# Weight sums of the input projections: stored from GpSimd's results for the second half, instead of made by adding transfers

## The chip, the cores and the metric

The kernel runs on one core of a Trainium2 chip. The metric is device time in microseconds of the slowest core, here the only one. Five engines work side by side, each in the order of its own queue: TensorE (PE in the profile, with its weight loads as PEld), VectorE (DVE), ScalarE (ACT), GpSimd (POOL) and SyncE (SP). SP, ACT and POOL also issue transfers, which 16 shared DMA engines carry out. A transfer issued by POOL can add its data to what lies at the destination; the kernel uses such adding transfers from DRAM to DRAM.

## What is computed

One layer of a hybrid trunk over 2048 positions of width 1024, in float32. Cut to what matters here:

```python
xn = rmsnorm(x, norm1_g)
z = xn @ w_in                      # pool | q | forget | input | output gate | branch gates
u_pool, zq, zf, zi, zo, zg = split(z)
gates = sigmoid(zg + b_gate)
ya = pool_mixer(u_pool) @ w_pa     # trailing means, per group a 128x128 product
yb = hgrn2_mixer(zq, zf, zi, zo) @ w_pb   # gated linear recurrence over chunks
x = x + (gates[0] * ya + gates[1] * yb) @ w_o
h = causal_conv3(rmsnorm(x, norm2_g) @ w_up)
x = x + (silu(gate_half(h)) * value_half(h)) @ w_down
out = rmsnorm(x, final_g)
```

## The kernel before

The sequence goes through in two halves of 1024 positions (b0 = 0 and b0 = 2), each as two blocks of 512. In each half the stages follow each other: the projections of the values and output gates ("io"), the other input projections in 14 units ("in": forget and q, branch gates, pool channels), the recurrence beside them in its own tasks, the two branch products (pa, pb), the output product (wo), the up product with its convolution and gating (up, 22 units), and the down product (dn).

The large products use a form of Strassen's scheme with seven half-size products, P1 to P7, in place of eight. P1, P2 and P4 take a quarter of the weights as it stands; P5, P6, P7 and P3 take sums and differences of quarters, called s1 to s4. Both operands are split into a rounded part and its remainder (ACT casts, VectorE subtracts), and three matmuls are made per pair; so every weight operand is one load into a raw buffer (line 183, on SP), a cast on ACT (L205) and a subtraction on VectorE (L206) into an operand buffer. There are 8 raw buffers and 6 operand buffers; loads run ahead as far as the raw buffers allow, conversions up to 4 operands ahead.

Where the sums s1 to s4 come from differs by half. The weights of wo, up and dn get their sums from adding transfers throughout: `Sums.make` takes a group of up to four units and issues eight transfers per group, four plain ones on ACT (L267) and four adding ones on POOL (L264), each of n x 256 KB for n units. `prepare` is a task that runs the groups two at a time, some seven ticks between the steps of a group, from the end of the first io stage on. A tick is six matmuls in program order, so the adding transfers spread over the first half. The input projections are needed first, before any such sums can be there: in the first half they load the quarters and add them on GpSimd (L373 for the "in" units, L315 for "io", there partly on VectorE). For the second half, `prepare` makes their sums again by transfers, as its last five groups: so0 (four units of io), si0, si1, si3 (four units each) and si2 (two units). Each sum in DRAM is then loaded like a quarter.

In the down product, POOL also issues the loads of its activations (g, L777) and of the residual rows (ac, L777), while SP issues the weight loads, then at its end the rows of x for the next half (L482) and the results (L1430). ACT squares those rows of x (L607) and casts the activations (dn_P, L578) in one queue.

The order of instructions on each engine is set by a scheduler from the program's text; so a change in one place moves neighbours elsewhere a little. The scheduler also gives every transfer one of eight completion counters: SP and ACT share eight, POOL has eight of its own. A transfer waits until the one eight places ahead of it on its set of counters has landed.

Of the kernel before, what the change touches and what calls it, by code (L numbers as in the profile page):

```python
# [11 lines left out]
F32 = mybir.dt.float32  # L12
# [6 lines left out]
P = 128  # L19
# [8 lines left out]
MF = D_FF // P  # L28
# [51 lines left out]
def tile_trunk(  # L80
# [77 lines left out]
    class Stream:  # L158
# [34 lines left out]
        def convert(self):  # L193
            j = len(self.tiles)
            key, fn, raws = self.ops[j]
            while any(r.tile is None for r in raws):
                self.load()
            v = fn(f"w{j}")
            t = opsp.tile([P, 2, 512], F32R, tag="ops", name=f"ops{j}")
            n = int(np.prod(v.shape[1:]))  # L200
            hi, lo = t[:, 0, :n], t[:, 1, :n]
            if len(v.shape) == 3:
                hi = hi.rearrange("p (a b) -> p a b", a=v.shape[1])
                lo = lo.rearrange("p (a b) -> p a b", a=v.shape[1])
            self.mark = act.copy(hi, v)  # L205
            dve.tensor_tensor(lo, v, f32(hi), ALU.subtract)  # L206
            self.tiles.append((key, t))
            self.load_ahead()
# [70 lines left out]
    def grouped(src, mv, mg, names):  # L279
# [7 lines left out]
        return names, [part(mv, 0), part(mv, 1), part(mg, 0), part(mg, 1)]  # L287

    def plan_one(key, src):
        r = stream.raw(src)  # L290
# [4 lines left out]
    def plan_io(b0):  # L295
        for p in IO_ORDER:
            for k in range(4):
# [6 lines left out]
                if b0:  # L304
                    plan_one("io", sums["io"].of(k, SUM_OF[p]))
                    continue
                use = {"P6": (2, 3, 0), "P5": (2, 3), "P7": (2, 0), "P3": (2, 3, 0, 1)}[p]
                raws = [stream.raw(q[i]) for i in use]

                def fn(nm, p=p, raws=raws):  # L310
                    t = raws[0].tile
                    for i, r in enumerate(raws[1:]):
                        t2 = slot(f"{nm}s{i}")
                        (dve if i == (p == "P6") and p != "P5" and p != "P7" else pool
                         ).tensor_tensor(t2, t, r.tile, ALU.add)  # L315
                        t = t2
                    return t

                stream.op("io", fn, raws)

    def plan_unit(key, src, kind, i, order, b0):
        mv, mg = proj_tiles(kind, i)
        if b0:
            unit = sums_of_unit(src, mv, mg, sums["in"], (kind, i))
        else:
            unit = weights_of_unit(src[mv], src[mg])
        for p in order:
# [23 lines left out]

    def sums_of_unit(src, mv, mg, made, unit):
        q = quarters(src[mv], src[mg])
        one = {"P1": q[0], "P2": q[1], "P4": q[3]}

        def plan(p):
            r = stream.raw(one[p] if p in one else made.of(unit, SUM_OF[p]))
            return (lambda nm: r.tile), [r]

        return {p: (lambda p=p: plan(p)) for p in ORDER}  # L360

    def weights_of_unit(src_v, src_g):
        src = quarters(src_v, src_g)
# [7 lines left out]
        def comb(nm, key, x0, x1):  # L371
            t = slot(f"{nm}{key}")
            pool.tensor_tensor(t, x0, x1, ALU.add)  # L373
            tmp[key] = t
            return t

# [27 lines left out]
    def plan_ffn():  # L404
        units = {}
        for m, p in up_order():
            if m not in units:
                units[m] = sums_of_unit(w_up_t, m, MF + m, sums["up"], m)
            fn, raws = units[m][p]()
# [24 lines left out]

    def group_in(kind, i0, n):
        mv, mg = zip(*(proj_tiles(kind, i) for i in range(i0, i0 + n + 1)))
        return grouped(w_in_t, mv, mg, [(kind, i) for i in range(i0, i0 + n)])

    prep = []

    def prepare():
        todo = [sums[name].make(g) for name in ("wo", "up", "dn", "io", "in")
                for g in range(len(sums[name].groups))]
# [12 lines left out]
    def group_rows(src, k0, n):  # L456
        v = src[k0 : k0 + n].rearrange("k p c -> p k c")
        return list(range(k0, k0 + n)), [v[:, :, c * 512 : (c + 1) * 512] for c in R_Q]

    io_q = w_io.rearrange("k p c -> p k c")  # L460
    sums["up"] = Sums("su", [group_up(m0) for m0 in range(0, MF, GROUP)])
    sums["wo"] = Sums("sw", [group_rows(w_o, 0, KD // 2)])
    sums["dn"] = Sums("sd", [group_rows(w_dn, k, min(GROUP, MF // 2 - k))
                             for k in range(0, MF // 2, GROUP)])
    sums["io"] = Sums("so", [(list(range(4)),
                              [io_q[:, :, c * 512 : (c + 1) * 512] for c in (0, 3, 1, 2)])])
    sums["in"] = Sums("si", [group_in(*g) for g in (("fq", 0, 4), ("g", 0, 4), ("u", 0, 2),
                                                    ("g", 4, 4))])

    for n in range(SEQ // SB):  # L470
# [1090 lines left out]
```

## Time and profile before

| | |
|---|---|
| time, median of 3 runs | 2723.14 us (2713.98, 2723.14, 2723.79) |
| the profiled execution's own time | 2727.51 us |
| its span | 2725.0 us |
| mean granted TensorE clock | 0.977 |
| busy: PE, DVE, ACT, POOL | 2568.9, 1990.4, 1166.1, 963.7 us |
| moved by DMA | 515.75 MB |
| of it by SP's, POOL's, ACT's queue | 301.01, 129.52, 82.96 MB |

The page's first part gives each engine's busy time; a share of 94% for PE says that its idle stretches, and the stretches at a lower granted clock, are what is left to gain without changing the products. The timeline of PE names after each idle stretch, in brackets, its length and the instruction that ended it. The windows view gives the busy time of each engine in chosen stretches, then the granted clock, the mean busy share of the DMA engines and GB/s. By the views of the tiles so and si the five groups' transfers lie between 1068 us, where ACT issues the first copy of so0, and 1492 us, where POOL issues the last adding transfer of si3; the down product of the first half runs from about 1165 to 1408 us and the second half's from about 2495 us to the end.

### The profile page before, as it was taken

The numbers are of one execution on the slowest core, as the hardware profiler recorded it, in microseconds if no ns is written. First come the engines' busy times: TensorE is split into PE (matmuls) and PEld (weight loads), VectorE is DVE, ScalarE is ACT, GpSimd is POOL, SyncE is SP. The second block draws the span as 40 slices with busy tenths as digits, with TensorE's granted clock in tenths as the row PEclk, the third lists the DMA queues.
The fourth block names the chain that finished last, engine by engine and source line by source line (L and its number), as shares of the span: only waits on it lengthen the run. The fifth ranks groups of instructions, "written<-read, shape, count | busy, mean of one in ns | idle before, by whom it ended". The sixth has DMA issues, their size and how long they took to land. (4 is left out here: it accounts for less than half of the span.)

```text
span 2725.0 us, 35432 instructions
## 1 busy us (share of the span) xinstructions
PE 2568.9 (94%) x11464; PEld 2077.4 (76%) x11464; DVE 1990.4 (73%) x3390; ACT 1166.1 (43%) x2204; POOL 963.7 (35%) x1273
## 2 busy tenths in 40 slices
PE   7899999889989999989989999999998899999998
PEld 6678887767767777768868788888786677777886
DVE  7888878358787777766577787675779777777744
ACT  5333434214544444444464344442355444444533
POOL 5544343061453343443253111201434323324402
PEclk8999999989989999999999999999999999999999
DMA  5656567889577788899888434346343443435942
GB/s 204 214 147 167 169 160 196 247 256 250 159 191 207 206 225 234 239 315 352 246 243 236 132 120 132 120 154 231 121 151 105 132 127 131 144 125 190 342 143 105
DMA packets 258313, 515.75 MB, mean 189 GB/s; under 512 B 26224, under 2 KB 42736, under 8 KB 257648
## 3 DMA queue, kind: packets, MB, share of 16 engines
q1 hardware_dynamic: 177600, 301.01, 34.1%
q0 software_dynamic: 51040, 129.52, 19.6%
q10 hardware_dynamic: 29488, 82.96, 8.6%
q8 instruction: 90, 1.47, 0.2%
q14 instruction: 95, 0.78, 0.1%
HBM read 422.69 MB, written 206.05 MB: 231 GB/s over the span
## 5 line engine op out<-in xcount | busy, mean ns | idle before, releaser
L205 ACT CAST ops<-raw 128x512 fp32r<-128x512 f32 x732 | 451.2, 620 | 932.6 <-PE up_Z L146 241.5
L206 DVE TENSOR_TENSOR ops<-raw,ops 128x512 fp32r<-128x512 f32 x732 | 563.4, 773 | 300.7 <-ACT ops L205 292.5
L1348 ACT ACTIVATE e<-h,cols 128x512 f32<-128x512 f32 x176 | 138.6, 813 | 19.3 <-DVE h L959 8.6
L1352 DVE SCALAR_TENSOR_TENSOR e<-h,cols,e 128x512 f32<-128x512 f32 x176 | 144.3, 825 | 0.0
L1065 POOL TENSOR_TENSOR gf_P<-e,e 128x512 f32<-128x512 f32 x44 | 77.8, 1769 | 171.8 <-DVE e L1358 113.0
L1350 DVE SCALAR_TENSOR_TENSOR e<-h,cols,e 128x512 f32<-128x512 f32 x176 | 134.6, 787 | 3.4
L777 POOL DMA_DIRECT2D g_P<-dg_P x154 | 86.2, 565 | 135.4 <-PE dn_P L146 49.5
L1343 POOL COPY h<-h 128x2 f32<-128x2 f32 x88 | 54.2, 642 | 152.8 <-DVE h L957 152.8
L1345 POOL COPY hist<-h 128x2 f32<-128x2 f32 x88 | 40.7, 462 | 180.3 <-DVE h L959 180.0
L146 PE MATMUL up_Z<-m_T30h,ops 128*128 128x512 f32 x88 | 39.6, 450 | 53.8 <-DVE up_u L995 53.8
L1276 POOL TENSOR_TENSOR ya<-ya,gl 128x512 f32<-128x512 f32 x32 | 46.2, 1473 | 112.0 <-DVE gl L1268 110.5
L999 DVE TENSOR_TENSOR up_u<-up_Z,up_e 128x512 f32<-128x512 f32 x44 | 30.4, 690 | 72.5 <-PE up_Z L146 72.4
L146 PEld LDWEIGHTS up_Z<-m_T30h,ops 128*128 128x128 f32 x88 | 17.2, 195 | 71.4 <-DVE up_u L995 38.1
L826 POOL COPY qm<-q 128x64 f32<-128x64 f32 x64 | 28.9, 462 | 118.2 <-DVE q L850 25.0
L1356 ACT ACTIVATE e<-e 128x512 f32<-128x512 f32 x88 | 54.9, 624 | 32.9 <-DVE e L1352 32.8
L1209 ACT ACTIVATE gt<-gt,cols 128x512 f32<-128x512 f32 x48 | 34.8, 725 | 78.8 <-DVE gt L959 61.3
L1172 POOL TENSOR_TENSOR q<-q,qs 128x512 f32<-128x512 f32 x16 | 21.9, 1371 | 127.4 <-ACT qs L1171 114.3
L1041 DVE TENSOR_TENSOR ac<-ac,dn_P 128x512 f32<-128x512 f32 x72 | 46.8, 682 | 27.7 <-PE dn_P L146 20.2
L959 DVE TENSOR_TENSOR h<-up_u,up_V 128x512 f32<-128x512 f32 x88 | 60.2, 684 | 5.4 <-PE up_V L146 3.9
L1065 POOL TENSOR_TENSOR gf_P<-gf_P,e 128x512 f32<-128x512 f32 x44 | 59.0, 1340 | 11.0 <-DVE e L1358 10.3
L1372 POOL DMA_DIRECT2D dg_P<-gf_P x88 | 55.6, 632 | 19.3 <-POOL gf_P L1065 18.7
L1041 DVE TENSOR_TENSOR x<-x,wo_P 128x512 f32<-128x512 f32 x88 | 56.1, 680 | 7.7 <-PE wo_P L146 7.6
(1270 smaller groups left out, 8367.7 us busy)
## 6 DMA issues: line engine op xcount, KB each, us to landing
g_P<-dg_P POOLq DMA_DIRECT2D x154, 256.0 KB, 7.1
raw<-in_w_up_t SPq DMA_DIRECT2D x132, 256.0 KB, 2.9
raw<-in_w_in_t SPq DMA_DIRECT2D x98, 256.0 KB, 2.9
dg_P<-gf_P POOLq DMA_DIRECT2D x88, 256.0 KB, 3.4
raw<-in_w_io SPq DMA_DIRECT2D x68, 256.0 KB, 5.2
dg_P<-e SPq DMA_DIRECT2D x66, 256.0 KB, 3.0
raw<-in_w_dn SPq DMA_DIRECT2D x66, 256.0 KB, 6.0
x<-in_x SPq DMA_DIRECT2D x64, 256.0 KB, 5.2
```

The costliest lines, as they stand in the source:

```text
L146: count[1] = pe.matmul(*args, **kw)
L205: self.mark = act.copy(hi, v)
L206: dve.tensor_tensor(lo, v, f32(hi), ALU.subtract)
L777: eng.dma_start(t, d)
L959: dve.tensor_tensor(dst, t, ps, ALU.add if how == "add" else ALU.subtract)
L1041: dve.tensor_tensor(t, t, ps[j], ALU.add if sg > 0 else ALU.subtract)
L1065: pin(pool.tensor_tensor(t, x0, x1, op))
L1348: act.activation(t, h[:, 2:], AF.Identity, bias=col(o_cb + mt), scale=col(o_cw + 4 * MF + mt))
L1350: dve.scalar_tensor_tensor(t, h[:, 1 : 1 + TB], col(o_cw + 2 * MF + mt), t, ALU.mult, ALU.add)
L1352: dve.scalar_tensor_tensor(t, h[:, 0:TB], col(o_cw + mt), t, ALU.mult, ALU.add)
L1356: act.activation(g, g, AF.Silu)
L1372: pool.dma_start(d, t)
```

## The change

The groups "io" and "in" are taken out of `prepare`: 20 adding transfers on POOL and 20 plain ones on ACT go. In the first half, each sum that GpSimd (or VectorE) has made for its own operand is also noted by `keep`, and `store_kept`, called at the start of the next operand's conversion, stores it to a DRAM tile of its own: 14 x 4 + 4 x 4 = 72 stores of 256 KB, all issued by SP. The second half loads from these tiles instead of from so and si. The number of loads, casts, subtractions and matmuls is the same.

```diff
--- before.py
+++ after.py
@@ -195,6 +195,7 @@
             key, fn, raws = self.ops[j]
             while any(r.tile is None for r in raws):
                 self.load()
+            store_kept()
             v = fn(f"w{j}")
             t = opsp.tile([P, 2, 512], F32R, tag="ops", name=f"ops{j}")
             n = int(np.prod(v.shape[1:]))
@@ -286,6 +287,18 @@
 
         return names, [part(mv, 0), part(mv, 1), part(mg, 0), part(mg, 1)]
 
+    kept, keeping = {}, []
+
+    def keep(key, t):
+
+        nm = "kw" + "".join(str(c) for c in np.ravel(key[1])) + f"{key[0]}{key[2]}"
+        kept[key] = dram.tile([P, 512], F32, tag=nm, name=nm)
+        keeping.append((kept[key], t))
+
+    def store_kept():
+        while keeping:
+            sp.dma_start(*keeping.pop(0))
+
     def plan_one(key, src):
         r = stream.raw(src)
         stream.op(key, lambda nm, r=r: r.tile, [r])
@@ -302,18 +315,19 @@
                     plan_one("io", q[one[p]])
                     continue
                 if b0:
-                    plan_one("io", sums["io"].of(k, SUM_OF[p]))
+                    plan_one("io", lambda k=k, p=p: kept["io", k, p])
                     continue
                 use = {"P6": (2, 3, 0), "P5": (2, 3), "P7": (2, 0), "P3": (2, 3, 0, 1)}[p]
                 raws = [stream.raw(q[i]) for i in use]
 
-                def fn(nm, p=p, raws=raws):
+                def fn(nm, k=k, p=p, raws=raws):
                     t = raws[0].tile
                     for i, r in enumerate(raws[1:]):
                         t2 = slot(f"{nm}s{i}")
                         (dve if i == (p == "P6") and p != "P5" and p != "P7" else pool
                          ).tensor_tensor(t2, t, r.tile, ALU.add)
                         t = t2
+                    keep(("io", k, p), t)
                     return t
 
                 stream.op("io", fn, raws)
@@ -321,9 +335,9 @@
     def plan_unit(key, src, kind, i, order, b0):
         mv, mg = proj_tiles(kind, i)
         if b0:
-            unit = sums_of_unit(src, mv, mg, sums["in"], (kind, i))
+            unit = sums_of_unit(src, mv, mg, lambda p: lambda: kept["in", (kind, i), SUM_OF[p]])
         else:
-            unit = weights_of_unit(src[mv], src[mg])
+            unit = weights_of_unit(src[mv], src[mg], (kind, i))
         for p in order:
             fn, raws = unit[p]()
             stream.op(key, fn, raws)
@@ -349,17 +363,17 @@
     def quarters(src_v, src_g):
         return [s[:, c * 512 : (c + 1) * 512] for s in (src_v, src_g) for c in range(2)]
 
-    def sums_of_unit(src, mv, mg, made, unit):
+    def sums_of_unit(src, mv, mg, made):
         q = quarters(src[mv], src[mg])
         one = {"P1": q[0], "P2": q[1], "P4": q[3]}
 
         def plan(p):
-            r = stream.raw(one[p] if p in one else made.of(unit, SUM_OF[p]))
+            r = stream.raw(one[p] if p in one else made(p))
             return (lambda nm: r.tile), [r]
 
         return {p: (lambda p=p: plan(p)) for p in ORDER}
 
-    def weights_of_unit(src_v, src_g):
+    def weights_of_unit(src_v, src_g, unit):
         src = quarters(src_v, src_g)
         raws, tmp = {}, {}
 
@@ -372,6 +386,7 @@
             t = slot(f"{nm}{key}")
             pool.tensor_tensor(t, x0, x1, ALU.add)
             tmp[key] = t
+            keep(("in", unit, key), t)
             return t
 
         def plan(p):
@@ -405,7 +420,8 @@
         units = {}
         for m, p in up_order():
             if m not in units:
-                units[m] = sums_of_unit(w_up_t, m, MF + m, sums["up"], m)
+                units[m] = sums_of_unit(w_up_t, m, MF + m,
+                                        lambda p, m=m: sums["up"].of(m, SUM_OF[p]))
             fn, raws = units[m][p]()
             stream.op("up", fn, raws)
         plan_rows("dn", w_dn, R_DN, MF // 2)
@@ -432,14 +448,10 @@
         ms = range(m0, m0 + n + 1)
         return grouped(w_up_t, ms, [MF + m for m in ms], list(range(m0, m0 + n)))
 
-    def group_in(kind, i0, n):
-        mv, mg = zip(*(proj_tiles(kind, i) for i in range(i0, i0 + n + 1)))
-        return grouped(w_in_t, mv, mg, [(kind, i) for i in range(i0, i0 + n)])
-
     prep = []
 
     def prepare():
-        todo = [sums[name].make(g) for name in ("wo", "up", "dn", "io", "in")
+        todo = [sums[name].make(g) for name in ("wo", "up", "dn")
                 for g in range(len(sums[name].groups))]
         active = []
         while todo or active:
@@ -457,16 +469,10 @@
         v = src[k0 : k0 + n].rearrange("k p c -> p k c")
         return list(range(k0, k0 + n)), [v[:, :, c * 512 : (c + 1) * 512] for c in R_Q]
 
-    io_q = w_io.rearrange("k p c -> p k c")
     sums["up"] = Sums("su", [group_up(m0) for m0 in range(0, MF, GROUP)])
     sums["wo"] = Sums("sw", [group_rows(w_o, 0, KD // 2)])
     sums["dn"] = Sums("sd", [group_rows(w_dn, k, min(GROUP, MF // 2 - k))
                              for k in range(0, MF // 2, GROUP)])
-    sums["io"] = Sums("so", [(list(range(4)),
-                              [io_q[:, :, c * 512 : (c + 1) * 512] for c in (0, 3, 1, 2)])])
-    sums["in"] = Sums("si", [group_in(*g) for g in (("fq", 0, 4), ("g", 0, 4), ("u", 0, 2),
-                                                    ("g", 4, 4))])
-
     for n in range(SEQ // SB):
         plan_mixer(n)
         plan_ffn()
```

The first place is POOL's queue in the first half's down product. Before, g0_P6_k is the activation k of product P6, ac0 the residual rows, si0s2 an adding transfer:

```order
L777 DMA g0_P6_5_10696<-dg0_P6_5_8731 128x512
L264 DMA si0s2_9744<-in_w_in_t 512x1x512
L777 DMA ac0_0_0_1_10719<-dx0_0_1_6071 128x512
L777 DMA ac0_0_1_1_10721<-dx0_1_1_6093 128x512
L777 DMA ac0_0_2_1_10723<-dx0_2_1_6128 128x512
L777 DMA ac0_0_3_1_10725<-dx0_3_1_6150 128x512
L777 DMA g0_P6_6_10727<-dg0_P6_6_9081 128x512
L777 DMA g0_P6_7_10750<-dg0_P6_7_9431 128x512
L777 DMA g0_P6_8_10773<-dg0_P6_8_9789 128x512
L777 DMA g0_P6_9_10813<-dg0_P6_9_10139 128x512
```

The same stretch with the change:

```order
L783 DMA g0_P6_5_10820<-dg0_P6_5_8875 128x512
L783 DMA ac0_0_0_1_10843<-dx0_0_1_6215 128x512
L783 DMA ac0_0_1_1_10845<-dx0_1_1_6237 128x512
L783 DMA ac0_0_2_1_10847<-dx0_2_1_6272 128x512
L783 DMA ac0_0_3_1_10849<-dx0_3_1_6294 128x512
L783 DMA g0_P6_6_10851<-dg0_P6_6_9225 128x512
L783 DMA g0_P6_7_10874<-dg0_P6_7_9575 128x512
L783 DMA g0_P6_8_10897<-dg0_P6_8_9923 128x512
L783 DMA g0_P6_9_10936<-dg0_P6_9_10269 128x512
```

The adding transfer is gone; the loads of g and ac follow each other in the same order.

The second place is SP's queue at the end of the first half's io stage, where the quarters of the last io operands (in_w_io) and the first units' weights (in_w_in_t) are loaded and zd and vd are results of the stage. Before:

```order
L183 DMA raw54_1114<-in_w_io 128x512
L183 DMA raw55_1116<-in_w_io 128x512
L183 DMA raw56_1139<-in_w_in_t 128x512
L183 DMA raw57_1141<-in_w_in_t 128x512
L183 DMA raw58_1143<-in_w_in_t 128x512
L183 DMA raw59_1145<-in_w_in_t 128x512
L183 DMA raw60_1174<-in_w_in_t 128x512
L1100 DMA zd0_0_286<-z0_0_0_1156 128x512
L183 DMA raw61_1176<-in_w_in_t 128x512
L183 DMA raw62_1178<-in_w_in_t 128x512
L183 DMA raw63_1180<-in_w_in_t 128x512
L1100 DMA zd0_0_286<-z0_0_1_1182 128x512
```

With the change; kw1ioP3 is the stored sum of io row block 1 for product P3, and w25s2 the tile in which GpSimd made it:

```order
L183 DMA raw54_1141<-in_w_io 128x512
L183 DMA raw55_1143<-in_w_io 128x512
L183 DMA raw56_1168<-in_w_in_t 128x512
L300 DMA kw1ioP3_1133<-w25s2_1131 128x512
L183 DMA raw57_1170<-in_w_in_t 128x512
L183 DMA raw58_1172<-in_w_in_t 128x512
L183 DMA raw59_1174<-in_w_in_t 128x512
L300 DMA kw2ioP3_1164<-w26s2_1162 128x512
L1106 DMA zd0_0_286<-z0_0_0_1185 128x512
L183 DMA raw60_1205<-in_w_in_t 128x512
L183 DMA raw61_1207<-in_w_in_t 128x512
L183 DMA raw62_1209<-in_w_in_t 128x512
```

Between the loads stand the stores, each of which waits on SP for GpSimd's sum; the loads of the next unit come behind it.

The third place is ACT's queue at the end of the first half's down product: the last activations of the product's last part (dn_P) and the squares of the second four row tiles of x. Before:

```order
L578 CAST dn0_P3_9h_12388<-g0_P3_9_12170 128x512
L607 ACTIVATE x3_xs0_0_12403,x3_0ss_12405<-x3_0_0_12372 128x512
L205 CAST ops406_12667<-raw392_12318 128x512
L607 ACTIVATE x3_xs0_1_12404,x3_0ss_12405<-x3_0_1_12374 128x512
L607 ACTIVATE x3_xs1_0_12414,x3_1ss_12416<-x3_1_0_12376 128x512
L607 ACTIVATE x3_xs1_1_12415,x3_1ss_12416<-x3_1_1_12378 128x512
L607 ACTIVATE x3_xs2_0_12425,x3_2ss_12427<-x3_2_0_12380 128x512
L607 ACTIVATE x3_xs2_1_12426,x3_2ss_12427<-x3_2_1_12382 128x512
L607 ACTIVATE x3_xs3_0_12436,x3_3ss_12438<-x3_3_0_12384 128x512
L607 ACTIVATE x3_xs3_1_12437,x3_3ss_12438<-x3_3_1_12386 128x512
L578 CAST dn0_P3_10h_12453<-g0_P3_10_12215 128x512
```

With the change:

```order
L584 CAST dn0_P3_9h_12486<-g0_P3_9_12270 128x512
L613 ACTIVATE x3_xs0_0_12501,x3_0ss_12503<-x3_0_0_12470 128x512
L613 ACTIVATE x3_xs0_1_12502,x3_0ss_12503<-x3_0_1_12472 128x512
L613 ACTIVATE x3_xs1_0_12512,x3_1ss_12514<-x3_1_0_12474 128x512
L613 ACTIVATE x3_xs1_1_12513,x3_1ss_12514<-x3_1_1_12476 128x512
L206 CAST ops405_12752<-raw391_12376 128x512
L613 ACTIVATE x3_xs2_0_12523,x3_2ss_12525<-x3_2_0_12478 128x512
L613 ACTIVATE x3_xs2_1_12524,x3_2ss_12525<-x3_2_1_12480 128x512
L613 ACTIVATE x3_xs3_0_12534,x3_3ss_12536<-x3_3_0_12482 128x512
L613 ACTIVATE x3_xs3_1_12535,x3_3ss_12536<-x3_3_1_12484 128x512
L584 CAST dn0_P3_10h_12551<-g0_P3_10_12314 128x512
```

The cast dn0_P3_10h stands behind all eight squares in both; only a cast of a weight operand has moved.

## The prediction

> **What bounds the kernel now.** I read the page's first part, then the windows view by stage, then PE's timeline in the stages where its busy share falls, then the queues of the engines it waits for there.
>
> ```profile
> PE 2568.9 (94%) x11464; PEld 2077.4 (76%) x11464; DVE 1990.4 (73%) x3390; ACT 1166.1 (43%) x2204; POOL 963.7 (35%) x1273
> 1100.00:1150.00 50.00, 47.94 (x207) 38.28 (x205) 40.21 (x57) 24.61 (x39) 19.84 (x27) 1.00 0.86 217
> 2200.00:2250.00 50.00, 47.95 (x207) 38.35 (x206) 40.28 (x57) 23.83 (x38) 16.36 (x24) 1.00 0.41 130
> ```
>
> PE is the bound. The change touches only what makes PE idle or slow. The two window rows (busy time and count of PE, PEld, DVE, ACT, POOL; then granted clock, DMA share, GB/s) are the same stage, the up product, in the first half with the adding transfers running and in the second without: 207 matmuls in 50 us in both, though the DMA engines are 86% and 41% busy. So in the up product these transfers cost nothing, and removing their first part (1068 to 1165 us) brings nothing there.
>
> The down product is different. The next rows are windows of its matmuls alone, first half and second, and of the transposes of x that share the first half's stretch:
>
> ```profile
> 1175.53:1408.00 232.47, 211.63 (x888) 169.02 (x888) 22.08 (x34) 0.96 0.94 296
> 2507.99:2707.00 199.01, 199.01 (x853) 161.47 (x854) 21.29 (x33) 0.99 0.60 210
> 1175.53:1408.00 232.47, 4.98 (x32) 4.17 (x32) 0.00 (x0) 3.21 (x6) 0.00 (x0) 0.96 0.94 296
> ```
>
> In the second half 853 matmuls take 199.01 us without a gap: 0.2333 us each. At that pace the first half's 888 take 207.2, with 5.0 for the transposes 212.2; the stretch lasts 232.5. So **20.3 us are lost in the first half's down product**, and the second half's, with the same loads but no adding transfers, is a control for the middle of the stage. PE's timeline says where; the bracket is the idle time and what ended it:
>
> ```profile
> 1175.53 2.10 PE L146 MATMUL dn_P<-ops,dn_P_3h 128*128 128x512 f32 x8 [1.75 <-ACT dn_P_3h L578]
> 1221.67 1.65 PE L146 MATMUL dn_P<-ops,dn_P_6h 128*128 128x512 f32 x3 [5.86 <-ACT dn_P_6h L578]
> 1380.92 2.12 PE L146 MATMUL dn_P<-ops,dn_P_7h 128*128 128x512 f32 x8 [1.15 <-ACT dn_P_7h L578]
> 1385.56 0.66 PE L627 MATMUL x_t<-ident,x_xs 128*128 128x128 f32 x4 [1.15 <-DVE x_xs L621]
> 1400.65 1.65 PE L146 MATMUL dn_P<-ops,dn_P_10h 128*128 128x512 f32 x3 [7.40 <-ACT dn_P_10h L578]
> 2507.99 1.58 PE L146 MATMUL dn_P<-ops,dn_P_3h 128*128 128x512 f32 x4 [3.97 <-ACT dn_P_3h L578]
> 1220.00:1230.00 10.00, 8.33 (x29) 6.68 (x30) 7.78 (x14) 5.91 (x11) 6.39 (x10) 0.74 1.02 334
> 1400.00:1410.00 10.00, 9.35 (x38) 7.76 (x39) 9.74 (x13) 6.24 (x13) 7.06 (x13) 0.69 0.38 61
> ```
>
> Two stalls matter, at 1221 and at 1400 us, and behind each the clock is at half for a while: 29 matmuls took 8.33 us instead of 6.8 (1.6 us more), and a mean clock of 0.69 over 10 us is 3.1 us of work lost, of which 0.3 fell into the idle time (2.8).
>
> **What the change does, part by part.**
>
> *The middle stall.* ACT came late to the cast that PE waited for, because of a weight load and then an activation load. The rows below are ACT's timeline, and the transfers issued at 1196 to 1222 us with their size and median time to landing; the last row is the same for the second half at 2528 to 2554.
>
> ```profile
> 1218.17 1.14 ACT L205 CAST ops<-raw 128x512 fp32r<-128x512 f32 x2 [7.47 <-DMA raw<-in_w_dn]
> 1221.00 0.62 ACT L578 CAST dn_P_6h<-g_P 128x512 fp32r<-128x512 f32 x1 [1.69 <-DMA g_P<-dg_P]
> g_P<-dg_P POOLq DMA_DIRECT2D x10, 256.0 KB, 10.8
> si0s<-in_w_in_t POOLq DMA_DIRECT2D x1, 1024.0 KB, 18.6
> so0s<-so0s ACTq DMA_DIRECT2D x1, 8.2
> g_P<-dg_P POOLq DMA_DIRECT2D x25, 256.0 KB, 6.8
> ```
>
> An addition of 1 MB to si0 and a copy within so0, both issued just before 1199 us, were under way, and the activations took 10.8 us to land instead of 6.8. With these gone, the place looks as in the second half, where no such gap stands. I take the whole stall with its half clock: 5.86 + 1.6 = **7.5 us gained**, bounds 0 (another load is late instead) and 7.5.
>
> *The stall at the end.* The cast dn_P_10h stands on ACT behind eight squares of the rows of x that SP loads for the next half, before and with the change (the third place above). So PE waits for the last of these loads. The rows: ACT's wait, the landing times of the first and the second eight loads of x, and SP's and POOL's queues (packets, MB, share of the 16 engines) at 1370 to 1402 us.
>
> ```profile
> 1393.22 0.63 ACT L607 ACTIVATE x_xs<-x 128x512 f32<-128x512 f32 x1 [3.06 <-DMA x<-in_x]
> DMA to landing us min/median/max: 4.2/5.4/6.0
> DMA to landing us min/median/max: 8.3/11.0/11.1
> q1 hardware_dynamic: 4667, 8.48, 73.9%
> q0 software_dynamic: 528, 1.05, 18.5%
> ```
>
> POOL's only large transfer there is one of si1, 1.05 MB, and it held 18.5% of the engines for 32 us: 5.9 us of all 16. Without it the last rows of x land up to 5.9 us earlier. The rest, SP's 8.48 MB with the 4 MB of x in it, stays, and so does the order on ACT. Of 1.15 + 1.15 + 7.40 = 9.7 us of stalls I take 5 us, and half of the 2.8 us of half clock: **6.4 us gained**. Bounds: 0, if x is held by its own burst, and 12.5.
>
> [...]
>
> *Issue time.* POOL and ACT lose the issue of 20 transfers each:
>
> ```profile
> L264 POOL DMA_DIRECT2D si0s<-in_w_in_t x4: 1169/1188/1227, 1118.3 to 1228.1; - x4
> L267 ACTq DMA_DIRECT2D si0s<-in_w_in_t x2: 550/564/577, 1077.1 to 1098.8; - x2
> ```
>
> 20 x 1.19 = 24 us and 20 x 0.56 = 11 us, spread over 420 us. POOL is busy a third of the time and PE's waits there are on loads, so I take 0. The upper bound is 3: the longest gap of PE in the first 100 us of the second half's projections, in the row below, and a half clock behind it, should they hang on POOL's or ACT's queue.
>
> ```profile
> 1518.23 0.50 PE L146 MATMUL gr_X<-x_f4h,ops 128*128 128x512 f32 x1 [1.64 <-ACT gr_e L993]
> ```
>
> The wait at the start of the down product (1.75 here, 3.97 in the second half without any adding transfers) stays: 0, bounds -2 and +2.
>
> *The 72 stores.* They are new in the first half's projections. The page's part 3 gives the price of bytes on each queue, the issue list a like store, SP's timeline one issue:
>
> ```profile
> q1 hardware_dynamic: 177600, 301.01, 34.1%
> q0 software_dynamic: 51040, 129.52, 19.6%
> q10 hardware_dynamic: 29488, 82.96, 8.6%
> dx<-x SPq DMA_DIRECT2D x32, 256.0 KB, 3.9
> 57.84 0.33 SPq L1092 DMA_DIRECT2D vd<-v  x1
> ```
>
> SP's queue took 34.1% of 2725 us for 301 MB: 3.1 us of all engines per MB, 0.81 us for a store of 0.262 MB, and 58 us for 72. (Removed are 18.9 MB on POOL's queue at 4.1 us and 18.9 MB on ACT's at 2.8: 131 us, so the sum of DMA work falls by 73.) Whether the 58 us show depends on what waits for loads where the stores fall:
>
> ```profile
> 60.00:130.00 70.00, 62.26 (x250) 48.30 (x249) 61.34 (x73) 27.72 (x48) 42.36 (x29) 0.95 0.70 225
> 130.00:480.00 350.00, 337.30 (x1671) 280.75 (x1670) 279.57 (x658) 131.16 (x296) 145.10 (x149) 0.98 0.63 169
> PE fr_Z L146 <- DVE ops L206: 2.7, 1, 2.7
> PE io_V L146 <- DVE ops L206: 2.1, 2, 1.1
> PE pl L873 <- DVE q L801: 3.6, 2, 2.5
> SPq L183 <- POOL w53s L373: 16.4, 1, 16.4
> ```
>
> The last four are waits: two of PE at 50 to 130 us, its longest at 130 to 480, and one of SP there. From 130 us on, where nearly all of the other 56 stores lie, no wait of PE is for a weight operand: its longest is on the recurrence. SP's loads already wait for GpSimd's sums, because the sum frees the raw buffer (16.4 us at w53s), and a store waits for that sum or an earlier one. So what is queued behind a store, the loads of the next units, waited that long before too. The cover is eight raw buffers, two units ahead; with it I take 0; the upper bound is 5, one issue time of 0.33 for each of 14 units. In the io stage there are 16 stores, and there PE does wait for weight operands (2.7, 2.1). Eight of the stores belong to the two products whose operands were late: 8 x 0.81 = 6.5 us if each delays its successor fully. VectorE is busy 61 of 70 us there, so that part of the delay hides: I take **3 us lost**, bounds 0 and 16 x 0.81 = 13.
>
> *Sum.* 7.5 + 6.4 - 3 = 10.9 us gained. From the profiled execution's 2727.5 that gives 2716.6. That execution lies 4.4 above the median of the runs shown, so I predict 2723.1 - 10.9 = **2712 us**.
>
> **The rivals.** *The whole loss goes.* The si1 transfer alone made the end late; then nearly all 20.3 us come back, less 1 for the stores: 2704. For it: x landed in 11 us instead of 5.4 exactly where si1 was under way. Against: eight loads of x at once, 2 MB, are a burst of their own.
>
> *Only the middle stall goes.* The end waits for x as before: 7.5 - 3 = 4.5, 2719. For it: the order on ACT is the same, and SP's queue held 8 MB in that stretch against POOL's one.
>
> *The stores hold up the first half.* One mechanism: SP takes its queue in order, a store waits for its sum, and the load behind it starts late by the store's issue and its share of the engines, 0.33 + 0.81 = 1.14 us. It decides where PE has no operand in reserve, the io stage: 16 x 1.14 = 18 us, with up to four half-clock stretches of some 1.6 = 25, against 13.9 gained: 11 us slower, 2734. If the reserve of the units is used up as well, 56 x 1.14 = 64 us more at most. It decides from 14 us of loss on. For it: the io stage's operands are late now. Against: VectorE sets its pace, and the DMA share of 0.70 leaves room.
>
> [...]
>
> **How the numbers follow.** My forecast has 50%, the whole loss back 20%, the middle stall alone 18%, the stores' rival 12%. This kernel can be told from no change at about 0.5%, 13.6 us. Two fifths of the forecast's half (its gains of 6 to 18) and the second case lie beyond it: 40% faster. Nearly all of the last case lies beyond it on the other side: 10% slower; 50% within. The forecast's own range is 2705 to 2717; with the other cases, the bounds of the stores and the spread of the runs, 2698 to 2726.
>
> **What would show it.** After the change, POOL's queue should move 110.6 MB, ACT's 64.1, SP's 319.9. The gap before dn_P_6h near 1221 us and its half clock should be gone, and the activations land in about 7 us. The gap before dn_P_10h should shrink to 2 or 3 us, with the second eight loads of x landing in 5 to 8. At 60 to 130 us the waits of PE on ops may grow by some 3 us, and at 130 to 480 none should appear. I am wrong if the io stage lengthens by over 8 us, if the end gap stays at 7, or if a new gap opens in the down product.

## The result and the profile after

The changed kernel takes **2705.57 us**, median of 4 runs (2703.0 to 2706.0), against 2723.47 for the kernel before (4 runs, 2713.98 to 2724.79). The ratio is 0.994, with a 95% interval from 0.9916 to 0.9963: 16 us faster, 10 to 23 by the interval. The prediction was 2712, with 2698 to 2726 as its range. The profiled execution took 2705.73 us, its span is 2704.0.

The page of the changed kernel, parts 1 and 3: busy time of PE, and the three queues that the change touches (packets, MB, share of the 16 engines).

```profile
PE 2558.7 (95%) x11464; PEld 2070.0 (77%) x11464; DVE 1998.2 (74%) x3390; ACT 1166.3 (43%) x2204; POOL 928.2 (34%) x1253
q1 hardware_dynamic: 187968, 319.89, 37.2%
q0 software_dynamic: 41504, 110.64, 15.9%
q10 hardware_dynamic: 24400, 64.08, 6.9%
```

The bytes moved as the change says: SP's queue carries the 72 stores, POOL's and ACT's have lost 18.9 MB each. PE's timeline in the two down products, and after it the matmuls of the first one from dn_P_3h to dn_P_10h in the windows view, first for the kernel before and then for the changed one:

```profile
1170.84 3.17 PE L146 MATMUL dn_P<-ops,dn_P_3h 128*128 128x512 f32 x8 [3.94 <-ACT dn_P_3h L584]
1382.02 2.38 PE L146 MATMUL dn_P<-ops,dn_P_10h 128*128 128x512 f32 x7 [3.77 <-ACT dn_P_10h L584]
2488.41 3.19 PE L146 MATMUL dn_P<-ops,dn_P_3h 128*128 128x512 f32 x8 [2.51 <-ACT dn_P_3h L584]
```

```profile
1175.53:1400.65 225.12, 206.14 (x876) 165.39 (x876) 20.96 (x32) 0.97 0.95 303
```

```profile
1170.84:1382.02 211.18, 205.22 (x877) 165.51 (x877) 20.84 (x32) 0.99 0.69 232
```

The same matmuls are busy for 206.1 and 205.2 us, but the stretch is 13.9 us shorter: the gap of 5.86 us near 1221 is gone, that of 7.40 before dn_P_10h is 3.77, the two of 1.15 between them are gone, and less time passes at half clock (a mean granted clock of 0.99 for 0.97). The gap at the start of the product went the other way, from 1.75 to 3.94.

The transfers issued in the middle of that product (1191 to 1217 us), and the landing of the second eight rows of x:

```profile
g_P<-dg_P POOLq DMA_DIRECT2D x25, 256.0 KB, 6.4
DMA to landing us min/median/max: 5.0/5.1/5.2
```

Before, the same 26 us held 10 loads of activations, landing in 10.8 us, and x landed in 11.0.

Where the 21 us between the two spans lie, by the starts of the same matmuls on PE's timeline, in us. The marks are the matmul with mxs_1h behind a wait of some 6 us, and the last up_Z with m_T30h that ends a wait of 2 us. The columns "again" are one more profile of each kernel; "removed" and "stores only" are the first two experiments below.

| stretch | before | again | after | again | removed | stores only |
|---|---|---|---|---|---|---|
| start to the branch products (mxs_1h) | 501.5 | 500.4 | 494.4 | 497.5 | 495.4 | 493.2 |
| to the last such up_Z with m_T30h | 632.8 | 630.5 | 631.6 | 630.5 | 631.3 | 631.5 |
| to dn_P_3h | 41.2 | 42.7 | 44.9 | 44.9 | 43.4 | 42.7 |
| to dn_P_10h | 225.1 | 224.6 | 211.2 | 211.9 | 212.7 | 225.1 |
| to the end of the span | 1324.4 | 1322.7 | 1322.0 | 1322.2 | 1319.8 | 1322.9 |

One row follows the adding transfers clearly: the down product, 225 with them and 212 without. The first row differs by up to 8 us between these kernels, and by 3 between two profiles of one.

### The profile page after: what moved, and what is told of

It is laid out like the page before. It is cut to its first block, busy times and chain, and to the rows that moved or that the text cites. A ratio compares the mean times of both kernels' runs of the same rounds, so it can differ in the third digit from the quotient of the medians.

```text
span 2704.0 us, 35550 instructions
## 1 busy us (share of the span) xinstructions
PE 2558.7 (95%) x11464; PEld 2070.0 (77%) x11464; DVE 1998.2 (74%) x3390; ACT 1166.3 (43%) x2204; POOL 928.2 (34%) x1253
```

## Experiments

**All of it out: neither stores nor adding transfers.** (In the second half a plain piece of weights takes the place of each sum.)

```diff
-                    plan_one("io", lambda k=k, p=p: kept["io", k, p])
+                    plan_one("io", q[0])
...
-            unit = sums_of_unit(src, mv, mg, lambda p: lambda: kept["in", (kind, i), SUM_OF[p]])
+            unit = sums_of_unit(src, mv, mg, lambda p: src[mv][:, :512])
...
-            store_kept()
```

> No stores, and none of the five groups of adding transfers: the second half's input projections take a plain 128x512 piece of the weights in the place of each sum, so their sums are left out. TensorE's order in the first half is that of the kernel before. Theory A (the adding transfers held back the loads of the down product, nothing else matters there): the stretch from dn_P_3h to dn_P_10h (before 225.1 us, after the change 211.2) is 209 to 213 here, with no gap before dn_P_6h. Theory B (the 7.1 us that the change brought ahead of 502 us belong to its new order): the projections reach mxs_1h at about 501 us as before, and the time is 2723 - 14 = 2709, some 4 above the change's 2705.6. Rival to B (the transfers removed make the projections faster by themselves, or the half clock ahead of 502 us is chance): 494 or so, and 2702 to 2705.

Measured: 2706.18 us (6 runs), ratio 0.9941 (0.9925 to 0.9957), the same as the changed kernel. The down product's stretch is 212.7, with no gap near 1221 and these at its ends:

```profile
1170.02 2.50 PE L146 MATMUL dn_P<-ops,dn_P_3h 128*128 128x512 f32 x5 [3.98 <-ACT dn_P_3h L582]
1382.68 1.66 PE L146 MATMUL dn_P<-ops,dn_P_10h 128*128 128x512 f32 x6 [3.35 <-ACT dn_P_10h L582]
```

So theory A holds, and the longer gap at the start comes with the removal, not with the stores. The branch products start at 495.4 although the order there is the old one: theory B falls.

**The stores alone, beside the adding transfers.**

```diff
+            store_kept()
...
+                    keep(("io", k, p), t)
...
+            keep(("in", unit, key), t)
```

(in the kernel before, with nothing reading the stored sums)

> The kernel before with the 72 stores added and read by nobody; the five groups of adding transfers and the loads of their sums stay. TensorE's order in the first half's projections is that of the changed kernel. Theory B (the order brings the 7.1 us): mxs_1h at 494 us, the down product's two stalls as before (5.9 and 7.4), 2723 - 7 = 2716. Rival (my prediction's term: the stores cost 3): mxs_1h at 504 and 2726. Rival (chance): mxs_1h anywhere from 494 to 504.

Measured: 2721.49 us (12 runs), ratio 0.9999 (0.9987 to 1.0012): the 72 stores cost nothing within 3.5 us. Both stalls are there as in the kernel before (6.07 and 6.32 us). Its profiled execution reached the branch products at 493.2 and took 2717, the other eleven runs 2715 to 2727, so what that one profile gained early is not the kernel's.

**Both kernels profiled again.**

> The kernel before, unchanged, profiled once more. If the half-clock stretches ahead of 502 us (at 126, 170, 256 and 420 us in the first profile) are this order's, they stand at the same places and mxs_1h starts at 500 to 503; if they are chance, some are gone and mxs_1h comes up to 7 us earlier. The stalls of 5.9 us at 1221 and 7.4 at 1400 should stand within 1 us in either case.

> The changed kernel profiled once more. If its lack of half clock between 127 and 492 us is its order's, mxs_1h starts at 493 to 496 again; if it is chance, some half-clock stretches are there and it starts up to 7 us later. The down product should again have one gap of about 3.8 us before dn_P_10h and one of about 3.9 before dn_P_3h.

Measured: branch products at 500.4 (before) and 497.5 (changed); the down product's gaps 4.90 and 7.21, and 3.94 and 3.88. The early gain of 7.1 us of the first pair of profiles is 2.8 in the second. The windows view of the changed kernel, first and second profile, over the same two pieces of work (1297 or 1296 matmuls, then 380 or 379), says what differs:

```profile
148.21:414.68 266.47, 255.64 (x1297) 211.93 (x1297) 223.59 (x512) 103.33 (x239) 118.40 (x124) 1.00 0.75 205
414.68:494.39 79.71, 72.94 (x380) 61.36 (x380) 56.72 (x148) 28.98 (x64) 18.45 (x21) 0.99 0.86 250
```

```profile
146.58:416.26 269.68, 258.26 (x1296) 214.27 (x1297) 222.85 (x512) 103.48 (x239) 117.10 (x124) 0.99 0.74 202
416.26:497.52 81.26, 74.35 (x379) 62.76 (x379) 56.70 (x148) 29.01 (x64) 17.60 (x20) 0.96 0.84 246
```

3.2 and 1.6 us more for one and the same program, at a granted clock of 0.99 for 1.00 and 0.96 for 0.99. So how much of a stretch passes at half clock is not fixed by the program.

**Two of the five groups made by adding transfers again (so, si0), then the other three (si1, si2, si3).** The first line is the first kernel's, beside so; the second line is the second kernel's.

```diff
+    sums["in"] = Sums("si", [group_in(*g) for g in (('fq', 0, 4),)])
...
+    sums["in"] = Sums("si", [group_in(*g) for g in (('g', 0, 4), ('u', 0, 2), ('g', 4, 4))])
```

> The changed kernel with the first two of the five groups (so and si0, 1.5 of the 5 by bytes) made by adding transfers again, at their old place; the other three come from stores. Theory A1 (so and si0 make the stall in the middle of the down product, si1 the one at its end): a gap of 5 to 6 us before dn_P_6h as in the three profiles with all the transfers (5.86, 4.90, 6.07), and before dn_P_10h one of 3.4 to 3.9 as in the three without any; the stretch from dn_P_3h to dn_P_10h is 211.5 + 7 = 218 to 219, the time 2705.6 + 7 - 2 (the wait at the start of the down product goes back from 3.9 to 1.75) = 2711. Rival A2 (any transfer beside the down product does a share of both): both gaps at about half, the same 2711. Rival A3 (the end is moved by the stall in the middle, whose delay makes the loads of x meet other loads): gaps of 5.5 and 7, 225 and 2718.

> The changed kernel with the other three groups (before's si1, si2, si3, which here carry the names si0, si1, si2) made by adding transfers again, at their old place from about 1230 us on, and so and si0 from stores. Theory A1 (si1's 1 MB holds the rows of x): no gap before dn_P_6h, and 6.3 to 7.4 us before dn_P_10h; the stretch from dn_P_3h to dn_P_10h is 211.5 + 4 to 6 = 216 to 218, the time 2710 to 2712. Rival A3 (the end goes with the middle) and the rival that x's own burst makes the end stall: 3.4 to 3.9 before dn_P_10h, 212 and 2706.

Measured: with the first two, 2720.25 us, ratio 0.9997 (0.9983 to 1.001); with the other three, 2711.09, ratio 0.9956 (0.9942 to 0.9971). PE's timeline of the first kernel:

```profile
1220.77 1.65 PE L146 MATMUL dn_P<-ops,dn_P_6h 128*128 128x512 f32 x3 [9.00 <-ACT dn_P_6h L597]
1393.44 1.89 PE L146 MATMUL dn_P<-ops,dn_P_10h 128*128 128x512 f32 x7 [3.22 <-ACT dn_P_10h L597]
```

and of the second:

```profile
1366.79 2.51 PE L146 MATMUL dn_P<-ops,dn_P_7h 128*128 128x512 f32 x8 [3.25 <-ACT dn_P_7h L601]
1386.94 2.50 PE L146 MATMUL dn_P<-ops,dn_P_10h 128*128 128x512 f32 x5 [7.58 <-ACT dn_P_10h L601]
```

Each set brings back its own stall and leaves the other at the size it has without transfers (3.2 at the end in the first; none near 1221 in the second): A1 holds, A2 and A3 fall. The sizes were missed: the stretch is 221.8 and 220.0 us, so the sets cost 10.6 and 8.8 apart and only 13.9 together. In the first, PE waits 9.0 us where it waited 5 to 6: it comes there 15.5 us behind the issue of the addition to si0, for 17.1 in the kernel before, and the load that it waits for took 19.2 us to land, for 13.8. In the second a gap of 3.25 appears at dn_P_7h, behind the first eight loads of x. I read this as a time put off by one stall that is partly spared at the next; no run shows it by itself. The time of the first was missed too, 2720 for 2711 expected: besides this stretch its profile is 6 us longer from the branch products to the last up_Z (637.6, in the table 630.5 to 632.8), and why is open.

**Each sum stored twice.**

```diff
+        keeping.append((dram.tile([P, 512], F32, tag="x" + nm, name="x" + nm), t))
```

> The changed kernel with each of the 72 sums stored a second time, to a place that nobody reads: 144 stores. Theory (stores cost nothing where VectorE and TensorE set the pace, as the 72 idle ones added to the kernel before showed: ratio 0.9999): 2705.6, within 4, the io stage ending as in the changed kernel at 123 to 124 us. Rival (my term: 3 us for 72, from the eight io stores that are next to late operands): 2709. Rival (a store delays the load behind it by 0.33 + 0.81 us once the buffers ahead are used up): 72 x 1.14 = 82 us at most, and half of it, 2746, if the reserve covers half.

Measured: 2724.83 us (12 runs), ratio 1.0002 (0.9987 to 1.0018): 17 to 19 us lost against the changed kernel, all of it ahead of the branch products (516.7). The first 72 stores are free (ratio 0.9999 for the stores alone), the second 72 are not. The next experiment asks for which reason.

**Each sum stored twice, the second time 8 columns only.**

```diff
+        keeping.append((dram.tile([P, 8], F32, tag="x" + nm, name="x" + nm), t[:, :8]))
```

> The changed kernel with a second store of each of the 72 sums, of 8 columns in place of 512 (4 KB in place of 256). 144 stores wait and are issued on SP as with the doubled stores, which cost 19 us, but hardly any bytes are added. Theory F (bytes: the doubled stores raise the share of the DMA engines from 0.77 to 0.83 at 148 to 517 us, and reloads on the recurrence's path land later): 2705 to 2708, mxs_1h at 494 to 498. Rival G (SP's queue in its order, each second store a wait and an issue of 0.33 us ahead of the loads): 2718 to 2725, mxs_1h at 508 to 517.

Measured: 2720.55 us (12 runs), ratio 0.9999 (0.9986 to 1.0012), branch products at 511.6. With 0.3 MB more instead of 19 nearly the whole loss is there, so it is not the bytes: F falls. The trace names something that G did not have. GpSimd, VectorE and PE one after the other, near 390 us:

```profile
388.40 1.06 POOL L757 TENSOR_TENSOR s<-s 128x524 f32<-128x524 f32 x1 [12.28 <-DMA xkwg4ins<-w98s]
389.50 0.69 DVE L1006 TENSOR_TENSOR gr_u<-gr_Z,gr_e 128x512 f32<-128x512 f32 x1 [6.24 <-POOL s L757]
390.24 0.72 PE L146 MATMUL gr_Z<-x_T40h,ops 128*128 128x512 f32 x1 [4.67 <-DVE gr_u L1006]
```

and in the changed kernel the same steps of GpSimd and PE, with the step of VectorE that takes the tile of w98s there:

```profile
374.14 1.06 POOL L756 TENSOR_TENSOR s<-s 128x524 f32<-128x524 f32 x1 [5.03 <-PE pv L914]
375.97 0.35 DVE L922 SCALAR_TENSOR_TENSOR ss<-st,f,pv 128x128 f32<-128x128 f32 x1 [5.92 <-DMA kwg4ins<-w98s]
378.74 0.50 PE L146 MATMUL gr_Z<-x_T40h,ops 128*128 128x512 f32 x1 [0.20 <-DVE gr_u L1005]
```

A sum's tile is one of 77 that all work shares, and it is free again only when the last store of it has landed. Here the pool branch's next tile is that of w98s, and GpSimd stands 12.3 us for its second store, which SP issued behind another load at 376.6 and which took 11.7 us to land. Then VectorE and PE wait in their turn. In the changed kernel the one store of w98s holds its tile too: VectorE stands 5.92 us for it, but PE's next wait there is only 0.20. So the first 72 stores also make others wait, and what differs is that the wait does not reach PE. How much of the 15 us comes by tiles held and how much by SP's later issues these runs don't separate; the order of the work also moved a little.

**The second block of x loaded and squared one part earlier.**

```diff
-X_AT, X_AT2 = 1, 4
+X_AT, X_AT2 = 1, 3
```

> The changed kernel with the second block of the rows of x for the next half loaded and squared one part of the down product earlier. Theory (the 3.8 us that are left before dn_P_10h are the wait of ACT's squares for x, whose eight loads are a burst of their own): that gap falls under 1.5 us with its half clock; 2705.6 - 2.5 - up to 1.7 = 2701 to 2703. Rival (the burst makes the same gap one part earlier, where the loads of that part's activations are late instead): a gap of 3 to 4 us some 16 us earlier, and 2705 to 2706.

Measured: 2702.73 us (6 runs), ratio 0.9932 (0.9914 to 0.995), not told apart from the changed kernel's 0.994. The gap moved, as the rival said:

```profile
1378.89 1.65 PE L146 MATMUL dn_P<-ops,dn_P_9h 128*128 128x512 f32 x3 [3.52 <-ACT dn_P_9h L584]
```

**The second block of x loaded one part earlier, squared at the old place.**

```diff
-X_AT, X_AT2 = 1, 4
+X_AT, X_LOAD2, X_AT2 = 1, 3, 4
...
+            if k == X_LOAD2 and not last:
+                load_rows(b0 + 3)
             if k == X_AT2 and not last:
-                load_rows(b0 + 3)
+                rows_ready(b0 + 3)
```

> The changed kernel, with the second eight loads of x issued one part of the down product earlier and their squares left at the old place. With loads and squares both earlier the gap of 3.8 us only moved from dn_P_10h to dn_P_9h (3.5). Theory E (ACT reaches the squares 3.1 us before x has landed; the lead is what lacks): ACT finds x in place, the gaps before dn_P_9h and dn_P_10h are both under 1.2 us, the stretch from dn_P_3h to the end of the part is 3 to 5 us shorter, 2701 to 2703. Rival (the burst of 2 MB delays something else, the activations' loads or the weights of the next half): a gap of 2 us or more at another operand within 20 us, and 2704 to 2706.

Measured: 2710.18 us (8 runs), ratio 0.9958 (0.9939 to 0.9976). The gap before dn_P_10h fell from 3.77 to 1.73, and the stretch from 211.2 to 209.7: less than half of theory E's gain.

```profile
1383.72 2.13 PE L146 MATMUL dn_P<-ops,dn_P_10h 128*128 128x512 f32 x8 [1.73 <-ACT dn_P_10h L587]
```

That the kernel is not faster is a slip of the edit: it also held back the squares of the very first rows of x until all of them had been loaded, and the second group of transposes came at 50.5 us instead of 45.5. These 5 us are in every run of it and in those of the combination below.

**The last three sums of activations on VectorE.**

```diff
-            pin(pool.tensor_tensor(t, x0, x1, op))
+            pin((eng or pool).tensor_tensor(t, x0, x1, op))
...
+                    dve if k == MF // 2 - 1 and m == MF - 1 else None)))
```

> The changed kernel, with the three last sums of activations of each half (gf, GpSimd's TENSOR_TENSOR at 1165.3, 1167.8 and 1171.2 us in the changed kernel's trace) made by VectorE. It asks why the wait at the start of the down product grew from 1.75 to 3.9 us with the transfers gone. Theory D (VectorE's two operations on e, 0.75 us each elsewhere, took 3.95 us together because GpSimd worked on its sums at the same time; ACT's last Silu waits for them and the cast dn_P_3h stands behind it): the pair takes 1.5 us, the gap before dn_P_3h falls to 3.9 - 2.4 + 0.7 for a sum that is now ahead on VectorE = 2.2 or less, in both halves, 2 to 4 us off the time with the half clock: 2702 to 2704. Rival (the pair is slow for another reason, or the wait is PE's arrival): the gap stays at 3.9 and the time at 2705.6.

Measured: 2700.14 us (4 runs), ratio 0.9931 (0.9907 to 0.9955), the fastest median here, though its interval overlaps that of the changed kernel. The gap before dn_P_3h is 1.75 in both halves. GpSimd's sum and VectorE's pair of operations in the changed kernel:

```profile
1165.30 1.60 POOL L1071 TENSOR_TENSOR gf_P<-e,e 128x512 f32<-128x512 f32 x1 [3.90 <-DVE e L1366]
1165.67 3.95 DVE L1358 SCALAR_TENSOR_TENSOR e<-h,cols,e 128x512 f32<-128x512 f32 x2
1169.65 0.63 ACT L1362 ACTIVATE e<-e 128x512 f32<-128x512 f32 x1 [2.09 <-DVE e L1358]
```

and the pair and PE's waits with the sums on VectorE:

```profile
1166.02 1.40 DVE L1359 SCALAR_TENSOR_TENSOR e<-h,cols,e 128x512 f32<-128x512 f32 x2
1169.00 2.12 PE L146 MATMUL dn_P<-ops,dn_P_3h 128*128 128x512 f32 x8 [1.75 <-ACT dn_P_3h L584]
2483.30 2.13 PE L146 MATMUL dn_P<-ops,dn_P_3h 128*128 128x512 f32 x8 [1.75 <-ACT dn_P_3h L584]
```

Theory D holds: 3.95 us beside GpSimd's sums, 1.40 without. GpSimd's sum began 0.37 us ahead of the pair (1165.30 and 1165.67 us), and the pair took 2.55 us longer than with the sums on VectorE. By what the two engines hold each other up, no run here shows.

**Both together,** with x ahead, the sums on VectorE, and these sums called after the down product's first row block.

> The changed kernel with x loaded ahead as in the run beside it, the three last sums of activations of each half on VectorE, and these sums called after the down product's first row block, by which ACT's cast dn_P_3h comes ahead of its last two Silus. Theory D and E together: no gap over 1.5 us at the start of the down product in either half and none at its end, 4 + 2.5 + 3 and up to three half clocks of 1.7: 2696 to 2700. If the half clock and the spread between runs cover it: 2702 to 2706.

Measured: 2703.68 us (6 runs), ratio 0.994 (0.992 to 0.996). The largest gap of PE in either half's down product is 1.23 us, and from the last up_Z with m_T30h to the second half's gr_X it takes 365.3 us for the changed kernel's 373.6; 5 of these 8 us are given back by the late start.

## Why the prediction came out as it did

**The largest part of the sum was right; the total was some 5 us too small.** Gained by the two stalls: 7.5 + 6.4 = 13.9 forecast, 13.9 measured (225.1 to 211.2), and 11.9 to 13.9 over the other pairs of the table. That the two agree to a tenth is luck: the measured stretch ends where dn_P_10h starts, so the 1.4 us forecast for the half clock behind it are not in it, and the idle time fell by 5.9 and 5.9 where I took 5.9 and 5. In all I forecast 10.9; the ratio says 16, with 10 to 23 as its interval. Of the 5 us between, 3 are the term of the stores; the other 2 lie within that interval.

**The middle stall: size right, cause half right.** I read it as loads that landed late (10.8 us) because two transfers of 1 MB shared the engines. Late loads did end it. The cast dn_P_6h waits for a load that POOL issued at 1207.2 us; by the views of line 777 at 1207.1 to 1207.4 and of the transfers issued at 1199 to 1211, all in the kernel before:

```profile
  ACT dn_P_6h L578: 1.7, 1
DMA to landing us min/median/max: 13.8/13.8/13.8
```

```profile
si0s<-in_w_in_t POOLq DMA_DIRECT2D x1, 1024.0 KB, 18.6
ac<-dx POOLq DMA_DIRECT2D x4, 256.0 KB, 17.9
raw<-in_w_dn SPq DMA_DIRECT2D x4, 256.0 KB, 9.3
g_P<-dg_P POOLq DMA_DIRECT2D x3, 256.0 KB, 13.8
```

In the other three profiles with this addition the load for dn_P_6h took 13.8, 13.2 and, with so and si0 alone, 19.2 us. Sharing the engines is not the whole reason: SP's loads of the same size, issued in the same 12 us, landed in 9.3 (medians). POOL's seven loads stand behind the addition on POOL's own DMA queue. The addition was issued at 1198.7 and landed at 1217.3; the seven were issued at 1199.4 to 1210.0, and none landed before it, but all in the 8 us after it. So I read the place behind this transfer of 1 MB as what counted most.

Waits on the issuing engines, which the prediction leaves out, lie over this. ACT's and then POOL's timeline, where ACTq and POOL's DMA rows are issues:

```profile
1210.08 0.62 ACT L205 CAST ops<-raw 128x512 fp32r<-128x512 f32 x1
1217.30 0.48 ACTq L267 DMA_DIRECT2D si0s<-si0s  x1
1218.17 1.14 ACT L205 CAST ops<-raw 128x512 fp32r<-128x512 f32 x2 [7.47 <-DMA raw<-in_w_dn]
```

```profile
1198.67 1.23 POOL L264 DMA_DIRECT2D si0s<-in_w_in_t  x1
1217.56 0.55 POOL L777 DMA_DIRECT2D g_P<-dg_P  x1 [7.01 <-DMA si0s<-in_w_in_t]
```

On ACT, the copy si0s<-si0s, which reads the addition's result, stood at the head of the queue until 1217.3, with the casts of two weight operands and then dn_P_6h behind it. On POOL, a load of activations stood 7.0 us until the addition had landed: it is the eighth transfer after the addition, the one that by the counters has to wait for it. It is not the load that dn_P_6h waits for. ACT was through with the two casts at 1219.3 and then waited 1.7 us more for that load, so its queue by itself would have kept PE waiting most of the time, but the loads ended the wait. In the run with so and si0 alone this is plainer: ACT's casts, which waited for the addition as well, are done at 1214.4, and dn_P_6h comes 5.7 us later, when its load has landed:

```profile
1212.73 0.47 ACTq L268 DMA_DIRECT2D si0s<-si0s  x1
1213.30 1.14 ACT L206 CAST ops<-raw 128x512 fp32r<-128x512 f32 x2 [6.84 <-DMA si0s<-in_w_in_t]
1220.10 0.62 ACT L597 CAST dn_P_6h<-g_P 128x512 fp32r<-128x512 f32 x1 [5.66 <-DMA g_P<-dg_P]
```

No run here moved the copy or the loads to another queue, so the division between the shared engines, POOL's DMA queue and ACT's is read from traces, not shown by a change.

**The stall at the end: right, and near its size.** It belongs to the late groups, as the run with them shows; that among them it is si1 is read from the traces, where no other large addition is under way. I forecast 5 of 9.7 us of waiting; gone are 5.9 (9.7 to 3.77). The gap of 2 to 3 us that I named as a sign is 3.77 all the same: the two gaps of 1.15 went whole, and less of the large one. The second eight rows of x land in 5.1 us instead of 11.0, at the good end of the 5 to 8 that I named. What is left is ACT reaching the squares before x: loading ahead takes it to 1.73.

**The start of the down product: the term was 0, within ±2, and it lost 2.2 in the gap.** I took the wait for one that stays, and didn't ask why the two halves differed (1.75 and 3.97). VectorE's timeline of the kernel before, first half:

```profile
1171.37 0.75 DVE L1352 SCALAR_TENSOR_TENSOR e<-h,cols,e 128x512 f32<-128x512 f32 x1
1172.03 0.69 DVE L1360 TENSOR_TENSOR e<-e,e 128x512 f32<-128x512 f32 x1
1172.63 0.75 DVE L1352 SCALAR_TENSOR_TENSOR e<-h,cols,e 128x512 f32<-128x512 f32 x1
```

Here the pair stands on both sides of the multiplication that lets GpSimd's sum begin, and its second operation starts ahead of that sum. With the transfers gone the scheduler gives the first half the order that the second had: the pair comes together, behind a subtraction, and meets GpSimd (3.95 us at 1165.67, as in the second half of the kernel before at 2502.82). In the second half the wait went the other way, 3.97 to 2.51. Together this is 0.7 us lost.

**The stores: 3 us lost forecast, 0 measured, within 3.5.** At 60 to 130 us the changed kernel's 253 matmuls are as many as the 250 before, though the share of the DMA engines rose from 0.70 to 0.81:

```profile
60.00:130.00 70.00, 62.76 (x253) 49.57 (x252) 62.40 (x74) 27.62 (x48) 41.93 (x29) 0.93 0.81 277
```

So the part of the delay that I let show hides as well. The step that failed is the price of a delayed operand in the io stage. PE's waits at 50 to 130 us add up to 9.2 us before and 8.7 after: those for weight operands fell from 5.8 to 2.9, where I expected some 3 more, and one for VectorE's io_u grew from 1.9 to 4.3. VectorE is busy for 62.4 of the 70 us, so I read it as the pace that covers the delay; no run changes that pace to show it. The rival in which the stores hold up the first half did not come true at 72 stores, and does at 144, though in part by something that it did not name, the tile that a store keeps occupied.

**The two rivals on the other side of the sum** are told apart by the same rows: the end stall did shrink, so "only the middle" is wrong, and 12 to 14 of the 20.3 us lost in the down product came back, not nearly all.

**What remains open** is the first 500 us. In the first pair of profiles the changed kernel gained 7.1 there, in the second 2.8; the runs without stores (495.4) and with stores beside the transfers (493.2) lie at the same end, and the medians of many runs allow the order with the stores no gain or loss over 3.5. I take it for chance of the clock, since the windows show the same work at 0.96 to 1.00 in one program, but an advantage of 1 or 2 us can't be excluded.

## To carry to other kernels

The addition of 1 MB took 18.6 us to land, and PE waited 5.86 us for a load of 256 KB that stood behind it. So before counting a transfer's bytes, look at which loads follow it on its own DMA queue, what waits for it on the issuing engine, and at who is behind that. A store of a sum kept its tile until it had landed (11.7 us for the second one of w98s); it was free as long as the wait for that tile did not reach PE, which bounds here (0.20 us of wait there with one store of each sum, 4.67 with the small second one), and doubling the stores is a cheap way to find how far away that is. Compare single profiles only where the same stretch repeats within them: the row that follows the edit in every pair is the effect, the others are spread.

## What had not been expected of the hardware

**The half clock depended on more than the length of the wait.** Two waits of the same length in one profile, the changed kernel's, on PE's timeline, and the windows of the 5 us behind each, with the granted clock as the last but two figure:

```profile
1084.62 0.50 PE L146 MATMUL up_Z<-m_T30h,ops 128*128 128x512 f32 x1 [2.07 <-DVE up_u L1001]
1125.98 0.50 PE L146 MATMUL up_Z<-m_T30h,ops 128*128 128x512 f32 x1 [2.06 <-DVE up_u L1001]
```

```profile
1084.60:1089.60 5.00, 4.98 (x22) 4.06 (x23) 3.43 (x4) 0.62 (x1) 1.84 (x4) 1.00 0.61 214
1126.00:1131.00 5.00, 5.00 (x15) 3.97 (x16) 2.02 (x2) 0.48 (x1) 1.81 (x4) 0.66 0.58 210
```

22 matmuls follow the one and 15 the other. Windows of 1 us show the clock at 0.50 from 1128 to 1130 us. So a wait of 2.06 us was followed by half clock here and one of 2.07 was not; what decides between them, no run shows.

**The stalls did not add.** In one profile each, the two sets of transfers cost 10.6 and 8.8 us apart, and 13.9 together.
